# A two-block transformer kernel on one core: the S5 products with C issued four at a time into column groups, and the first attention's logits of two heads in turn on the halves of the rows

## The chip, the cores and the metric

The kernel runs on one core of a Trainium2 chip, as one launch. The metric is the device time of one execution in microseconds; lower is better. The host only lays the arrays out beforehand.

## The reference

Two transformer blocks run one after the other on 256 tokens of width 2048, in float32. Each has a wide input projection, several mixers, gates, an output projection and an MLP with a squared ReLU. What matters here are two mixers:

```
# block 1: attention with forget gates, 8 heads of 64
log_f  = log_sigmoid(f_logit + f_bias);  cum = cumsum(log_f)          # per token and head
logits = einsum('bqhd,bkhd->bhqk', q_block, k) * 64 ** -0.5
logits = logits + (cum[q] - cum[key]);  masked;  softmax;  @ v        # query blocks of 128

# block 2: S5, 64 groups of 16 channels, each with 64 complex states
s = scan(a, einsum('blgh,gph->blgp', u, bb))                          # complex, over the tokens
y = einsum('blgp,ghp->blgh', s_re, c_re) - einsum('blgp,ghp->blgh', s_im, c_im)
```

## The kernel before

Activations are kept transposed: features on the 128 partitions, tokens on the free axis. The bulk of the work is a stream of weight products. `run_stream` goes through 1048 steps; in step i ScalarE casts a 512 x 256 block of weights to its high part and VectorE subtracts it to get the low part (`split_step(i + 3)`, tile `w`, four buffers), evacuations that are due are issued (`run_late`), and TensorE multiplies the block of step i (`mm_step`, tile `ps`). Then `run_mixers` issues pieces of two generators, `chain_a` and `chain_b`, until a budget of VectorE time (1.42 us a step) is used up. So the order in each engine's queue is fixed when the program is built, and the mixers' products stand in TensorE's queue between steps of the stream.

A float32 product of the mixers is two passes on TensorE: the trace counts two MATMULs for each `mm` whose operands are plain float32, and one for each whose operands are float32r. All below count passes.

`attn1`, in `chain_a`, takes two heads at a time, r = 0 to 3. For each head hh of the pair it forms the logits in a bank of its own (`mx` tiles): for the two query blocks a product q k over 64 rows (head 0 on partitions 0 to 63, head 1 on 64 to 127), and a second product on the same columns that adds the row of minus the cumulated forget gates: a one-hot column of the identity against `ncr[0:8]`, over 8 rows. That is 16 passes for each r. `ncr` is made in `forget` from a product of 8 output columns, `pr`. Later in the same loop, the products with v of the two heads go to the two halves of one bank's partitions, each with 64 columns of stationary operand.

The S5 mixer, the second half of `chain_b`, goes through t = 0 to 31 (two groups each; kt = t // 4, q = t % 4). For each t VectorE rotates the inputs `bu` into `pa` and `pb`, runs two scans, and rotates back into `z0`, a `pz` tile out of two buffers. One t later, after the scans of t, `y(t - 1, z0)` multiplies it by 32 columns of C (`ct`), into partitions 32 q to 32 q + 31 of `yps`: two products, real and imaginary, four passes. Then `bu(t + 1)` follows, two passes. After four t VectorE reads `yps` (`y_out`), and GpSimd's queue loads the next `ct` when the old one is free, with the tables `tab` behind it.

`acc` and `sq2` are two tiles [128, 2, 256] that sum the squares for the norms; between the norm ahead of block 2 and the output projection of block 2 nothing else uses them.

Of the kernel before, what the change touches and what calls it, by code (L numbers as in the profile page):

```python
# [11 lines left out]
F32 = mybir.dt.float32  # L12
# [6 lines left out]
D = 2048          # model width  # L19
L = 256           # tokens  # L20
# [10 lines left out]
# Everything below keeps activations transposed: features on partitions, tokens on the free axis.  # L31
# A product x @ w with float32 accuracy takes three float32r passes: every operand is the exact sum
# of two float32r parts (hi, lo) and hi*hi + hi*lo + lo*hi is accumulated in PSUM.


class Group:
    """256 columns of a weight matrix against K rows, in steps of 512 rows.

    mode F: two accumulators, [w_hi x_hi + w_lo x_hi | w_hi x_lo]; T: the same with the tokens on the
    output partitions; M: one accumulator and 512 columns.  # L40
    """
# [7 lines left out]
class Build:  # L49
# [33 lines left out]
    def split(self, dst, k, n, src):  # L83
        """dst (r8 tile), k tiles k..k+n <- exact hi and lo parts of src [128, n, 256]."""
        hi = dst[:, k:k + n, 0]
        self.A.copy(hi, src)  # L86
        self.tt(dst[:, k:k + n, 1], src, hi.bitcast(F32), SUB)

    def split_scaled(self, dst, k, src, g):
        """dst k tile k <- parts of src [128, 256] times the per-partition g."""  # L90
        hi = dst[:, k, 0]
        self.act(hi, src, AF.Copy, scale=g)
        self.stt(dst[:, k, 1], src, g, hi.bitcast(F32), MUL, SUB)

# [164 lines left out]
    def first_work(self):  # L259
        """loads in the order of need, the split of x between those of the first weights"""  # L260
        I, S = self.I, self.S
        S.dma_start(self.T4[0], I["x"][0])
        S.dma_start(self.gs, I["gs"])
        self.load_unit(0, halves=True)
        self.V.memset(self.e32, E32)
        self.act(self.acc[:, 0, 0:32], self.e32, AF.Copy)
        S.dma_start(self.T4[1], I["x"][1])
        self.load_unit(1)
        S.dma_start(self.T4[2], I["x"][2])
        S.dma_start(self.T4[3], I["x"][3])  # L270
        S.dma_start(self.cst, I["cst"])
        self.load_unit(2)
        self.V.memset(self.mh, -0.5)
        self.open_b1()
        self.xg = self.R[0:4]
# [7 lines left out]
    def squares_x(self, j):  # L283
        """as squares(), on GpSimd: the other engines have no time for it at the start"""
        t = self.sgt("sqx")
        G = self.G
        G.tensor_tensor(t, self.T4[j], self.T4[j], op=MUL)
        if j == 0:
            G.tensor_tensor(self.acc, t[:, 0:2], t[:, 2:4], op=ADD)
        else:  # L290
            for h in range(2):
                G.tensor_tensor(self.acc, self.acc, t[:, 2 * h:2 * h + 2], op=ADD)
# [11 lines left out]
    def squares(self, x, first=False, last=False):  # L304
        """add x*x to acc; the last ones are left to the sum over the partitions"""
        if first:
            self.act(self.acc, x, AF.Square)
            return
        t = self.sq2 if last else self.ev("sq")
        self.act(t, x, AF.Square)  # L310
        if not last:
            self.tt(self.acc, self.acc, t, ADD)
# [4 lines left out]
    def norm(self, tag, fast=False):  # L317
        """rstd of the tokens, per token partition (rt) and as rows on all partitions (rbc)."""
# [30 lines left out]
    def hold(self, norm):  # L349
        """an evacuation waits for its norm, as long as the PSUM ring allows"""  # L350
        if norm not in self.have:
            self.held.append(norm)
            while norm not in self.have:
                yield 0.0
            self.held.remove(norm)

# [1 line left out]
    def ab(self, ps, name="ab"):  # L358
        """sum of the two accumulators"""
        t = self.ev(name)  # L360
        self.A.copy(t, ps[:, :, 1])  # L361
        self.tt(t, ps[:, :, 0], t, ADD)
        return t
# [60 lines left out]
    def evac_res(self, x, j, s, xg=None, gi=None, sq=True, flag=None, then=None):  # L424
        """x += product; then the parts of x*g for the next product and the squares for its norm"""
# [46 lines left out]
    def make_groups(self):  # L472
        R, T = self.R, self.T4
        # block 1
# [53 lines left out]
        # block 2  # L528
# [128 lines left out]
    def exp_acc(self, out, y, n):  # L657
        """exp(y) for [128, n] with a relative error of a few ulp"""
        self.G.tensor_tensor(out, self.e32[:, 0:n], y, op=ALU.pow)
        for _ in range(3):  # L660
            yield None
        t = self.p.tile([128, 32], F32, name="xa", tag="xa", bufs=1)[:, 0:n]
        self.ts(t, y, E32_FIX, 1.0, MUL, ADD)
        self.tt(out, out, t, MUL)

    def log1p_half(self, out, z, n):
        """log1p(z)/2 for 0 <= z <= 1, in place of an odd series in z/(2+z)"""
# [11 lines left out]
    # -- block 1  # L679
# [3 lines left out]
    def open_b1(self):  # L683
# [16 lines left out]
        self.cq, self.ncr, self.c2 = sm("cq", 16), sm("ncr", 256), sm("c2", 4)  # L700
        self.lf, self.rq, self.sm1 = sm("lf", 16), sm("rq", 32), sm("sm1", 32)
# [9 lines left out]
    def forget(self):  # L711
# [13 lines left out]
        # rows hi, lo of w by columns hi, lo of x: three of the four blocks add up to the product  # L725
# [26 lines left out]
        # coefficient of the recurrence, -4 softplus(-lambda)  # L752
# [16 lines left out]
        self.mm(pr[0:8, 0:128], lf[:, 0], self.U)  # L769
        self.mm(pr[0:8, 128:256], lf[:, 1], self.U, True, False)  # L770
        self.mm(pr[0:8, 128:256], lf[:, 0], self.ones, False, True)
        yield None
        self.V.tensor_copy(self.cq, ps[:, 0:16])
        self.act(self.ncr[0:8], pr[0:8, 0:256], AF.Copy, scale=-1.0)
# [102 lines left out]
    def attn1(self):  # L877
# [39 lines left out]
        for r in range(4):  # L917
            yield None
            pss = []
            for hh in range(2):  # L920
                h, hs = 2 * r + hh, slice(64 * hh, 64 * hh + 64)
                ps = self.mxt()
                hot = self.ident[0:8, h:h + 1].to_broadcast([8, 128])
                for o, ls, n in ((0, slice(0, 128), 128), (128, slice(128, 256), 256)):
                    self.mm(ps[:, o:o + n], q[hs, r, ls], kk[hs, r, 0:n], True, False)
                    self.mm(ps[:, o:o + n], hot, self.ncr[0:8, 0:n], False, True)
                pss.append(ps)
# [50 lines left out]
    # -- block 2  # L978
# [15 lines left out]
    def scatter(self, eng, dst, k, n, src):  # L994
        """[(q r), k, 256] of every src to its rows of dst [k, (src r), q, 256]"""
        for i, t in enumerate(src):
            for q in range(4):
                rs = slice(32 * q, 32 * q + 32)
                eng.dma_start(dst[k:k + n, 32 * i:32 * i + 32, q].rearrange("k r n -> r k n"), t[rs])

    def s5_params(self):
# [36 lines left out]
        # zero-order hold: k = (exp(lambda dt) - 1) / lambda  # L1038
# [55 lines left out]
        # exp(i theta t) for t < 256 by doubling, first 32 for all states at once  # L1094
# [110 lines left out]
    def gmlp(self):  # L1205
        # in the places of q and k, which the attention no longer needs
# [63 lines left out]
    def chain_b(self):  # L1270
        # The product with B contracts 16 channels only: the parts hi, lo of the input, for four
        # times 32 channels, go one below the other on 128 rows, and so do those of B
# [55 lines left out]
        def y(t, z):  # L1328
            kt, q = t // 4, t % 4
            if q == 0:  # L1330
                yps[kt] = self.p_mx.tile([128, 256], F32, name="yps", tag="yps", bufs=1)
            o = yps[kt][32 * q:32 * q + 32]
            for c in range(2):
                self.mm(o, ct[kt][:, c, q], z[:, c], c == 0, c == 1)
# [15 lines left out]
        z0 = None  # L1350
        for t in range(32):
# [14 lines left out]
            if t:  # L1366
                y(t - 1, z0)
# [6 lines left out]
            z0 = nt("pz", 2)  # L1374
# [11 lines left out]
        y(31, z0)  # L1386
# [31 lines left out]
def _tiles(w):  # L1418
    """[K, N] -> [N/512, 2, K/512] blocks of [128, 4, 256]: 512 rows by 256 columns, rows on partitions"""
# [5 lines left out]
def _cols(v):  # L1425
    """[n*128] -> [128, n]"""
# [3 lines left out]
def _layout(a):  # L1430
# [41 lines left out]
    sb = np.zeros((2, 64, 2, 32, 2, 16), f32)       # q, p, re/im, tau, q', channel  # L1472
    sc = np.zeros((8, 2, 64, 2, 4, 2, 16), f32)     # kt, q, p, re/im, tau%4, q', channel
# [27 lines left out]
```

## Time and profile before

| | |
|---|---|
| runs shown, median of 3 | 3115.57 us (3114.85 to 3116.56) |
| span of the profiled execution, first to last instruction | 3107.6 us |
| TensorE busy | 3079.1 us (99%) |
| VectorE busy | 2126.8 us (68%) |
| ScalarE busy | 1437.8 us (46%) |
| mean share of the 16 DMA engines, whole span | about 5 to 6 tenths |
| mean granted TensorE clock | 0.993 |

The page has the profiled execution's own time as its span alone; what lies around the span isn't in it. The median of the runs is 8.0 us above that span. A busy TensorE is one that has passes in flight; whether it gets through them at its best pace has to be read from starts of passes that follow each other.

### The profile page before, as it was taken

How to read it: one execution, taken by the hardware profiler on the slowest of the kernel's cores; microseconds unless marked ns; L12 is line 12 of the kernel's file. 1: busy time of each engine (PE TensorE's matmuls, PEld its weight loads, DVE VectorE, ACT ScalarE, POOL GpSimd, SP SyncE). 2: the span in 40 equal slices, each digit the busy share in tenths (PEclk: the TensorE clock that was granted, in tenths of full speed). 3: DMA queues.
4: the chain of work that ended last, by engine and by line, in shares of the span. 5: the costliest groups of instructions: out<-in, count | busy, mean ns of one | idle time of the engine just before them, and what ended most of it. 6: DMA issues, size and time to landing. Idle time of an engine off the chain costs nothing.

```text
span 3107.6 us, 43754 instructions
## 1 busy us (share of the span) xinstructions
PE 3079.1 (99%) x18072; PEld 2684.9 (86%) x18072; DVE 2126.8 (68%) x2607; ACT 1437.8 (46%) x1737; POOL 88.1 (3%) x115
## 2 busy tenths in 40 slices
PE   8999999999999999999999999999999999999998
PEld 6888889988888888888888888888998888888887
DVE  6765566566788976566678788886566656565565
ACT  4455444445544434344445554445444434344443
POOL 3000000000000000000000000000000000000000
PEclk9999999999999999999999999999999999999999
DMA  5554455565566665555675566655555555555553
GB/s 213 174 174 149 148 178 188 190 216 188 193 230 213 234 215 205 190 190 203 218 237 188 182 209 207 206 177 190 188 199 189 182 185 189 189 182 186 189 188 124
DMA packets 158567, 597.90 MB, mean 192 GB/s; under 512 B 11168, under 2 KB 13472, under 8 KB 158112
## 3 DMA queue, kind: packets, MB, share of 16 engines
q1 hardware_dynamic: 150464, 569.94, 52.9%
q0 software_dynamic: 7328, 24.12, 2.8%
q8 instruction: 142, 2.33, 0.3%
q10 hardware_dynamic: 576, 1.05, 0.1%
q14 instruction: 57, 0.47, 0.0%
HBM read 577.24 MB, written 17.83 MB: 191 GB/s over the span
## 4 chain that ended last, share of the span: by engine, by line
PE 75%; issue 23%; DVE 1%; DMA 0%; ACT 0%; SPq 0%; POOLq 0%; POOL 0%; DVEq 0%; ACTq 0%
PE ps L81 72%; PE mx L81 2%; PE yps L81 1%; PE bu L81 0%; DVE R L75 0%; DMA T<-in_x 0%; DVE w L66 0%; DVE T L66 0%; PE mx L958 0%; ACT w L130 0%; PE mx L1081 0%; SPq L117 0%; POOLq L1496 0%; POOL rt L315 0%; DVE ab L66 0%
## 5 line engine op out<-in xcount | busy, mean ns | idle before, releaser
L81 PE MATMUL ps<-R,w 128*128 128x256 f32 (+1 forms) x16768 | 2861.5, 333 | 15.0 <-DVE w L66 7.4
L81 PEld LDWEIGHTS ps<-R,w 128*128 128x128 f32 x16768 | 2507.7, 189 | 354.7 <-DVE w L66 8.8
L66 DVE TENSOR_TENSOR w<-raw,w 128x1024 fp32r<-128x1024 f32 x1048 | 1282.4, 1225 | 927.2 <-ACT w L130 926.4
L130 ACT CAST w<-raw 128x1024 fp32r<-128x1024 f32 x1048 | 1099.7, 1050 | 1557.0 <-PE ps L81 1383.2
L66 DVE TENSOR_TENSOR T<-T,ps 128x512 f32<-128x512 f32 x160 | 109.4, 684 | 9.1 <-PE ps L81 6.3
L81 PE MATMUL ps<-w,R 128*128 128x512 f32 (+1 forms) x640 | 114.2, 338 | 0.0
L81 PEld LDWEIGHTS ps<-w,R 128*128 128x128 f32 x640 | 97.5, 188 | 13.9
L66 DVE TENSOR_TENSOR ab<-ps,ab 128x512 f32<-128x512 f32 x154 | 105.3, 684 | 0.0
L361 ACT COPY ab<-ps 128x512 f32<-128x512 f32 x154 | 89.2, 579 | 0.0
L66 DVE TENSOR_TENSOR ab<-ab,rbc 128x512 f32<-128x512 f32 x120 | 83.1, 693 | 4.2
L315 POOL TENSOR_TENSOR rt<-nv,mh 128x2 f32<-128x2 f32 x5 | 3.5, 703 | 2022.7 <-DVE nv L72 2022.7
L66 DVE TENSOR_TENSOR R<-ab,R 128x512 fp32r<-128x512 f32 x68 | 46.6, 685 | 0.0
L86 ACT CAST R<-ab 128x512 fp32r<-128x512 f32 x68 | 41.8, 615 | 7.2 <-DVE ab L66 7.2
L75 DVE SCALAR_TENSOR_TENSOR ab<-ab 128x512 f32<-128x512 f32 x64 | 43.8, 684 | 0.0
L75 DVE SCALAR_TENSOR_TENSOR R<-T,gs,R 128x256 fp32r<-128x256 f32 x64 | 39.3, 660 | 4.0 <-ACT R L78 4.0
L1365 DVE TENSOR_TENSOR_SCAN pb<-magT,pa 128x256 f32<-128x256 f32 x64 | 40.7, 678 | 0.8
L78 ACT ACT_TABLE_LOAD x28 | 35.9, 1283 | 1.2 <-PEq L1492 0.7
L81 PE MATMUL yps<-pz,ct 128*32 128x256 f32 x128 | 33.6, 385 | 0.0
L78 ACT ACTIVATE R<-T,gs 128x256 fp32r<-128x256 f32 x64 | 28.5, 499 | 5.7 <-DMA T<-in_x 3.5
L1314 ACT CAST xs<-xk 128x256 fp32r<-128x256 f32 x32 | 12.9, 402 | 31.0 <-PE bu L81 29.9
L1307 POOL DMA_DIRECT2D tab<-dtab x32 | 17.7, 554 | 259.1 <-DVE pz L66 259.0
L66 DVE TENSOR_TENSOR pz<-pz,pa 128x256 f32<-128x256 f32 x64 | 24.2, 419 | 0.2
(217 smaller groups left out, 873.3 us busy)
## 6 DMA issues: line engine op xcount, KB each, us to landing
raw<-in_w_in SPq DMA_DIRECT2D x191, 1024.0 KB, 4.9
raw<-in_w_up SPq DMA_DIRECT2D x128, 1024.0 KB, 4.8
raw<-in_w_down SPq DMA_DIRECT2D x128, 1024.0 KB, 4.9
raw<-in_w_branch SPq DMA_DIRECT2D x40, 1024.0 KB, 4.9
raw<-in_w_out SPq DMA_DIRECT2D x32, 1024.0 KB, 4.9
dtab<-tb SPq DMA_DIRECT2D x16, 512.0 KB, 7.5
tab<-dtab POOLq DMA_DIRECT2D x32, 256.0 KB, 3.2
T<-in_x SPq DMA_DIRECT2D x8, 512.0 KB, 7.0
```

Of the source, the lines that this page charges most:

```text
L66: self.V.tensor_tensor(out, a, b, op=op)
L75: self.V.scalar_tensor_tensor(out, a, s, b, op0=op0, op1=op1)
L78: self.A.activation(out, a, func, **kw)
L81: self.T.matmul(out, lhsT, rhs, start=start, stop=stop, skip_group_check=True)
L86: self.A.copy(hi, src)
L130: self.A.copy(w[:, :, 0], raw)
L315: self.G.tensor_tensor(out, v, self.mh[:, 0:out.shape[-1]], op=ALU.pow)
L361: self.A.copy(t, ps[:, :, 1])
L1307: self.G.dma_start(tab[t], self.d_tab[t // 2][:, t % 2])
L1314: self.A.copy(xs[t], xk[kt][:, q])
L1365: self.V.tensor_tensor_scan(b[:, c], mg, a[:, c], 0.0, op0=MUL, op1=ADD)
```

## The change

It has two parts.

In S5, the states of four consecutive t are kept (`zs`), and when t % 4 is 0 and t is not, `y(kt - 1, zs)` issues the eight products of the four t at once: first the real parts of q = 0 to 3, then the imaginary ones, each q into its own 32 columns of the array. Since four states must live at once, q = 0 uses `acc`, q = 1 uses `sq2`, and q = 2 and 3 the two `pz` buffers.

In the first attention, both heads' products are issued in turn: q k of head 0 on rows 0 to 63, q k of head 1 on rows 64 to 127, then the two forget products. These now take 64 rows each, on the same halves: `ncr` is cleared to zero once, filled at partitions 0 to 7 and 64 to 71 (so `forget` makes `pr` twice and copies it twice), and the one-hot column is chosen on the half of its head.

Comments are taken out as well.

```diff
+        self.V.memset(self.ncr, 0.0)
...
-        self.mm(pr[0:8, 0:128], lf[:, 0], self.U)
-        self.mm(pr[0:8, 128:256], lf[:, 1], self.U, True, False)
-        self.mm(pr[0:8, 128:256], lf[:, 0], self.ones, False, True)
+        for o in (0, 64):
+            self.mm(pr[o:o + 8, 0:128], lf[:, 0], self.U)
+            self.mm(pr[o:o + 8, 128:256], lf[:, 1], self.U, True, False)
+            self.mm(pr[o:o + 8, 128:256], lf[:, 0], self.ones, False, True)
...
-        self.act(self.ncr[0:8], pr[0:8, 0:256], AF.Copy, scale=-1.0)
+        for o in (0, 64):
+            self.act(self.ncr[o:o + 8], pr[o:o + 8, 0:256], AF.Copy, scale=-1.0)
...
-            pss = []
-            for hh in range(2):
-                h, hs = 2 * r + hh, slice(64 * hh, 64 * hh + 64)
-                ps = self.mxt()
-                hot = self.ident[0:8, h:h + 1].to_broadcast([8, 128])
-                for o, ls, n in ((0, slice(0, 128), 128), (128, slice(128, 256), 256)):
-                    self.mm(ps[:, o:o + n], q[hs, r, ls], kk[hs, r, 0:n], True, False)
-                    self.mm(ps[:, o:o + n], hot, self.ncr[0:8, 0:n], False, True)
-                pss.append(ps)
+            pss = [self.mxt(), self.mxt()]
+            for o, ls, n in ((0, slice(0, 128), 128), (128, slice(128, 256), 256)):
+                for hh in range(2):
+                    hs = slice(64 * hh, 64 * hh + 64)
+                    self.mm(pss[hh][:, o:o + n], q[hs, r, ls], kk[hs, r, 0:n], True, False)
+                for hh in range(2):
+                    hs, h = slice(64 * hh, 64 * hh + 64), 64 * hh + 2 * r + hh
+                    hot = self.ident[hs, h:h + 1].to_broadcast([64, 128])
+                    self.mm(pss[hh][:, o:o + n], hot, self.ncr[hs, 0:n], False, True)
...
-        def y(t, z):
-            kt, q = t // 4, t % 4
-            if q == 0:
-                yps[kt] = self.p_mx.tile([128, 256], F32, name="yps", tag="yps", bufs=1)
-            o = yps[kt][32 * q:32 * q + 32]
+        def y(kt, zs):
+            yps[kt] = self.p_mx.tile([128, 256], F32, name="yps", tag="yps", bufs=1)
             for c in range(2):
-                self.mm(o, ct[kt][:, c, q], z[:, c], c == 0, c == 1)
+                for q, z in enumerate(zs):
+                    self.mm(yps[kt][32 * q:32 * q + 32], ct[kt][:, c, q], z[:, c], c == 0, c == 1)
...
-            if t:
-                y(t - 1, z0)
+            if t and q == 0:
+                y(kt - 1, zs)
+                zs = []
...
-            z0 = nt("pz", 2)
+            z0 = (self.acc, self.sq2)[q] if q < 2 else nt("pz", 2)
+            zs.append(z0)
...
-        y(31, z0)
+        y(7, zs)
```

On TensorE, the logits of one r (the second, r = 1) stand like this before; `mx<-T,T` is a product q k, `mx<-ncr,cst` one with the forget row, `ps` is the stream, and the size is that of the output:

```order
L81 MATMUL ps_2308<-R_74,w_2212 128x256
L81 MATMUL mx<-T_83,T_82 128x128
L81 MATMUL mx<-ncr,cst 128x128
L81 MATMUL mx<-T_83,T_82 128x256
L81 MATMUL mx<-ncr,cst 128x256
L81 MATMUL mx<-T_83,T_82 128x128
L81 MATMUL mx<-ncr,cst 128x128
L81 MATMUL mx<-T_83,T_82 128x256
L81 MATMUL mx<-ncr,cst 128x256
L81 MATMUL ps_2308<-R_75,w_2233 128x512
```

And like this with the change, between the same two products of the stream:

```order
L81 MATMUL ps_2313<-R_74,w_2217 128x256
L81 MATMUL mx<-T_83,T_82 128x128 x2
L81 MATMUL mx<-ncr,cst 128x128 x2
L81 MATMUL mx<-T_83,T_82 128x256 x2
L81 MATMUL mx<-ncr,cst 128x256 x2
L81 MATMUL ps_2313<-R_75,w_2238 128x512
```

The number of products is the same; the two of each row are now those of head 0 and head 1.

On TensorE in S5, the product with C of t = 3 and its surroundings before:

```order
L81 MATMUL ps_13299<-R_81,w_13289 128x512
L81 MATMUL ps_13299<-R_81,w_13289 128x256
L81 MATMUL yps<-pz,ct 32x256 x2
L81 MATMUL bu<-xs,ws 128x256 x2
L81 MATMUL ps_13423<-R_75,w_13323 128x512
```

And the same place with the change (`sq_92` is `sq2`), where the products of t = 0 to 3 now all stand:

```order
L81 MATMUL ps_13295<-R_81,w_13285 128x512
L81 MATMUL ps_13295<-R_81,w_13285 128x256
L81 MATMUL yps<-acc,ct 32x256
L81 MATMUL yps<-sq_92,ct 32x256
L81 MATMUL yps<-pz,ct 32x256 x2
L81 MATMUL yps<-acc,ct 32x256
L81 MATMUL yps<-sq_92,ct 32x256
L81 MATMUL yps<-pz,ct 32x256 x2
L81 MATMUL bu<-xs,ws 128x256 x2
L81 MATMUL ps_13426<-R_75,w_13319 128x512
```

At the three places ahead of this one, t = 0 to 2, the `yps` row is gone and `bu` follows the stream directly. Beside these places the queues of all engines hold the same instructions in the same order, apart from the names of the state tiles, one more MEMSET on VectorE at the start, and in `forget` three more products and one more copy on ScalarE.

## Rows read from the trace of the kernel before

**Rows 1.** Page: the span; the chain that ended last, by engine.

```profile
span 3107.6 us, 43754 instructions
...
PE 75%; issue 23%; DVE 1%; DMA 0%; ACT 0%; SPq 0%; POOLq 0%; POOL 0%; DVEq 0%; ACTq 0%
```

**Rows 2.** Waits of TensorE, whole span: total us, times, longest us.

```profile
PE ps L81 <- DVE w L66: 7.4, 3, 3.8
PE ps L81 <- ACT w L130: 7.3, 1, 7.3
```

**Rows 3.** Chain that ended last, in S5: start us, us, what (passes).

```profile
1583.69 0.24 PE bu L81 x2
...
1600.19 0.98 PE yps L81 x4
1601.17 0.43 PE bu L81 x2
...
2073.10 0.98 PE yps L81 x4
```

**Rows 4.** Chain that ended last, at the logits and one product with v.

```profile
255.15 4.15 PE mx L81 x16
...
279.93 0.81 PE mx L81 x8
...
322.50 5.09 PE mx L81 x16
...
359.62 4.68 PE mx L81 x16
```

**Rows 5.** TensorE in order of time, logits of r = 0: start us, us, passes.

```profile
255.08 0.49 PE L81 MATMUL mx<-T,T 64*128 64x128 f32 x2
255.49 0.48 PE L81 MATMUL mx<-ncr,cst 8*128 8x128 f32 x2
255.90 0.70 PE L81 MATMUL mx<-T,T 64*128 64x256 f32 x2
256.53 0.69 PE L81 MATMUL mx<-ncr,cst 8*128 8x256 f32 x2
```

**Rows 6.** Tile scr on TensorE: the products with v.

```profile
L81 PE MATMUL mx<-scr,T x32: 272/326/430, 279.9 to 390.8; 128*64 128x256 f32 x16, 128*64 128x128 f32 x16
```

**Rows 7.** In order of time, up to 279.8605, then up to 279.8725: passes begun.

```profile
279.86 0.43 PE L81 MATMUL mx<-scr,T 128*64 128x256 f32 x1
...
279.86 0.44 PE L81 MATMUL mx<-scr,T 128*64 128x256 f32 x2
```

**Rows 8.** Stretches at and after logits: busy us (instructions) by engine, granted clock, DMA.

```profile
255.00:259.20 4.20, 4.20 (x18) 2.34 (x16) 1.88 (x3) 1.04 (x1) 0.00 (x0) 1.00 0.25 52
...
291.30:294.70 3.40, 3.40 (x13) 2.83 (x12) 1.35 (x4) 0.00 (x0) 0.00 (x0) 0.51 0.00 0
...
325.50:332.30 6.80, 6.80 (x19) 4.82 (x20) 1.87 (x6) 0.00 (x0) 0.00 (x0) 0.50 0.13 53
...
363.10:369.80 6.70, 6.70 (x20) 5.28 (x20) 1.83 (x5) 0.00 (x0) 0.00 (x0) 0.50 0.05 19
```

**Rows 9.** S5 stretches: PE, PEld, DVE, ACT, POOL, clock, DMA.

```profile
1580.00:2080.00 500.00, 498.34 (x3008) 425.54 (x3007) 419.03 (x609) 252.70 (x342) 36.39 (x67) 1.00 0.59 197
1840.00:1960.00 120.00, 120.00 (x782) 105.00 (x781) 106.33 (x155) 59.01 (x81) 10.67 (x19) 1.00 0.60 203
```

**Rows 10.** In order of time, all engines, after the product of t = 19.

```profile
1914.83 1.05 PE L81 MATMUL yps<-pz,ct 128*32 128x256 f32 x4
...
1916.36 0.68 DVE L66 TENSOR_TENSOR pz<-pb,tab 128x512 f32<-128x512 f32 x1
```

**Rows 11.** In order of time, in forget, and VectorE at the start.

```profile
81.32 0.82 PE L81 MATMUL mx<-cst,lf 128*8 128x128 f32 x6
...
82.18 0.37 ACT L78 ACTIVATE ncr<-mx 8x256 f32<-8x256 f32 x1 [0.28 <-PE mx L81]
...
4.97 3.63 DVE L75 SCALAR_TENSOR_TENSOR R<-T,gs,R 128x256 fp32r<-128x256 f32 x4 [3.81 <-ACT R L78]
```

More of the change, by code (lines that the diff above doesn't have):

```diff
@@ L1349, in chain_b @@
         yield None
-        z0 = None
+        zs = []
         for t in range(32):
@@ L1365, in chain_b @@
                 self.V.tensor_tensor_scan(b[:, c], mg, a[:, c], 0.0, op0=MUL, op1=ADD)
-            if t:
-                y(t - 1, z0)
+            if t and q == 0:
+                y(kt - 1, zs)
+                zs = []
             if q == 0:
```

## The prediction

> **What bounds the kernel now.** I read the head of the page and its chain that ended last first: nearly all of that chain is TensorE, or issue time in which nothing is waited for [rows 1]. The waits of TensorE confirm it: its two largest sums are about 7 us each out of 3107.6 us, in four waits altogether [rows 2]. So the time is the length of TensorE's queue, and a change is worth what it takes out of that queue, at the place where it takes it, as long as VectorE keeps up.
>
> Then I read the chain at the two places of the change. In S5 every product with C stands in it: four passes take 0.98 us, and the `bu` behind takes 0.43 us where one with no such product ahead took 0.24 us [rows 3]. There are 32 of these products, each at 0.98. In the first attention the 16 passes of each r stand in it too, with 4.15 us for r = 0 and the same for r = 1, 5.09 for r = 2 and 4.68 for r = 3 [rows 4].
>
> **What one pass costs.** The logits of r = 0 in order of time give it [rows 5]. Two passes of 128 tokens go from one start to the next pair's in 0.41 us, two of 256 in 0.63. The 0.22 between them is two times 128 tokens, so a pass streams in 0.11 us per 128 tokens and 0.22 per 256. A pair of 128 then has 0.41 - 0.22 = 0.19 us that is no streaming, and it comes once for each pair, where the rows in use change from 64 to 8 or back. Check: 8 x 0.11 + 8 x 0.22 + 8 x 0.19 = 4.16, against 4.15. The S5 product fits as well: 4 x 0.22 = 0.88, and 0.10 of change on the way in; on the way out `bu` pays 0.43 - 0.24 = 0.19.
>
> **Do passes on different parts of the array run at once?** One place of the kernel before answers for columns. The products with v put two heads on the two 64-column halves, each with two passes of 256 and two of 128 tokens for every r [rows 6]. One after the other they would stream for 4 x 0.22 + 4 x 0.11 = 1.32 us; they took 0.81 with the changes included [rows 4]. And within 0.012 us of the first pass a second one of 256 tokens had begun [rows 7], which must be the other head's, since passes of one head can't start so close. The program writes all of head 0 ahead of head 1, so three unstarted passes were passed over.
>
> [...]
>
> **The change part by part.**
>
> S5. Removed: 32 x (0.98 + 0.19) = 37.4 us. In their place stand 8 batches of 16 passes, four in each column group. With the four groups at once a batch streams for 4 x 0.22 = 0.88, plus 0.10 on the way in, at most 0.04 for three later starts and 0.19 on the way out: 1.21 us, 9.7 in all. To start the fourth group TensorE must pass over three unstarted passes, as many as it did for v. Saved: 27.7 us. No row shows more than two groups, so the bounds are one pass at a time (16 x 0.22 + 0.29 = 3.8 us a batch, 30.5 in all, 6.9 saved) and all four. I take all four, since the groups are of the same kind as the two that the rows show.
>
> Logits. Removed: 4.15 + 4.15 + 5.09 + 4.68 = 18.1 us. All 16 passes now use 64 rows, so the seven changes inside an r go, and the two halves of the rows write two banks. With both halves at once an r takes 4 x 0.11 + 4 x 0.22 = 1.32, plus one change of 0.19: 1.5 us, 6.0 in all, 12.1 saved. Halves of rows never stand next to each other in the trace before; the nearest row is again that of v. The lower bound is nothing saved, if the 0.19 belongs to products on part of the rows and not to the change, and the halves take turns.
>
> Clock. [...] What r = 2 and 3 lost inside the logits is in the sum already (5.09 and 4.68); outside, half of 3.4, of 4.7 (327.6 to 332.3) and of 5.5 (364.3 to 369.8) is lost, 6.8 us. What TensorE did before each fall was some 3 to 4 us of passes on 64 or 8 rows. The S5 products, 1.2 us at a time, leave the clock at 1.00 throughout [rows 9]. At 1.5 us an r is nearer to these, so I take all 6.8 as saved, with 0 as the other bound.
>
> `forget`. Six passes of 8 columns are added to six that took 0.82 us; they lie in another column group, so I take 0.2 of at most 0.8. The second copy, 0.37 us on ScalarE [rows 11], delays only ScalarE there. The MEMSET falls in the first 5 us, where VectorE waits for its first input until 4.97 [rows 11]. Both at nothing.
>
> New waits. In S5 VectorE now writes `acc` at t = 4, 8, ... right after the batch that reads it was issued; the two-buffer `pz` gave it one t more. At t = 20, the tightest of these places, that write began at 1916.36, and the product of t = 19 had ended at 1914.83 + 0.98 = 1915.81 [rows 10]: 0.55 us to spare, of which the longer batch uses 0.04. Were it late, the next weight split would queue behind it on VectorE, and TensorE meets that only once its three steps of ready weights are used up. The next `ct` load waits for the end of the batch as it did for the last product, with the table loads behind it on GpSimd's queue, at most 0.04 us later.
>
> Sum: -27.7 - 12.1 - 6.8 + 0.2 = -46.4 us. The profiled span of 3107.6 would become 3061.2. The page gives no time around it; I leave the 8.0 us by which the median lies above the span as they are: 3115.6 - 46.4 = **3069.2 us**, 1.5% faster. A difference of under 0.2%, 6.2 us, would not be told from no change.
>
> **Rivals.**
>
> 1. Not all four column groups at once. If two at a time, a batch has 8 rounds of 0.22 and takes 2.1 us; if passes start strictly in order, both passes of q hold up q + 1, which makes 9 rounds, 2.3 us. 8 batches cost 16.6 or 18.2 us instead of 9.7: 3076 to 3078 us. The products with v speak against strict order, nothing speaks for or against four. [...] Chance 0.14.
>
> 2. Halves of rows take turns. Streaming stays 2.64 us and one change is left, 2.8 us for an r: 6.8 saved instead of 12.1, and between 0 and 6.8 of the clock, since runs of 2.8 us lie between those that lowered it and those that didn't: 3074 to 3081; with the 0.19 still paid by each pair, 3088. Chance 0.13; together with the first, 3081 to 3090, 0.05.
>
> 3. VectorE becomes the bound in S5. It is busy 419 of 500 us, and 106.3 of 120 in the fullest stretch [rows 9]; with 27.7 us less that is 89%, and with about 7 us less there 94%. Against it: no wait of TensorE for VectorE worth naming there, and 6% left. If the stretch from 1840 on (235 us) kept its pace, 13 us of the gain would be lost: 3082. Chance 0.05.
>
> 4. Slower: the clock. If passes neither overlap in columns nor in rows, a batch is 3.8 us of passes on 32 columns, as long as the logits that lowered the clock. A fall of 6.8 us after each of 8 batches costs 8 x 3.4 = 27 us against 6.9 saved; with logits at 2.8 us and their falls unchanged (-6.8), the end is 3115.6 - 6.9 + 27.2 - 6.8 = 3129. It decides from about five such falls on. Chance 0.03.
>
> **How the numbers follow.** The forecast has the remaining 0.60, with a range of its own of 3063 to 3074 (the clock's other falls shift by one or two, overheads of a batch are off by half a microsecond). The range for all is 3062 to 3088: it takes in the first three rivals and leaves out the fourth, the worst of the second and a bit below. Faster by over 0.2% is everything but the fourth and part of an unforeseen mix: 0.95; within 0.2%: 0.02; slower: 0.03.
>
> **What would show each step.** In the changed profile: 8 groups of 16 `yps` passes in the chain of about 1.0 us each, and `bu` at 0.24 behind the stream at the other 24 places; 16 `mx` passes in about 1.5 us for each r; a granted clock of 1.00 from 255 to 375 us; VectorE's share in S5 near 89% without new waits of TensorE. Batches of 2 us or logits of 2.8 would make the prediction wrong by the amounts above, and falls of the clock behind the batches by more.

## The result and the profile after

The change takes 3064.1 us (median of 4 runs, 3063.0 to 3076.2) against 3115.2 before (median of 4, 3101.8 to 3116.6); the ratio is 0.9855, 95% interval 0.9838 to 0.9872. The forecast was 3069.2. In four more runs of the change, with seven of before beside them, the ratio was 0.9849 (0.9824 to 0.9873). The profiled execution of the change has a span of 3074.1 us and took 3076.2, the longest of the first four. So 2.1 us lie around the span, not the 8.0 that the prediction left there, and the profiled execution of before stands for a run of about 3109.7.

The page still says that TensorE's queue is the time [rows 1]:

```profile
span 3074.1 us, 43760 instructions
...
PE 75%; issue 23%; DVE 1%; DMA 0%; ACT 0%; SPq 0%; POOLq 0%; POOL 0%; DVEq 0%; ACTq 0%
```

The chain that ended last, in S5 (start us, us, passes), to be read against [rows 3]:

```profile
1596.55 0.23 PE bu L81 x2
...
1632.44 1.00 PE yps L81 x16
1633.44 0.43 PE bu L81 x2
...
2040.37 1.00 PE yps L81 x16
```

Sixteen passes take 1.00 us where four took 0.98, and the chain has eight such pieces. `bu` without a product ahead of it takes 0.23 us.

TensorE in order of time at the first batch:

```profile
1632.37 0.40 PE L81 MATMUL yps<-acc,ct 128*32 128x256 f32 x1
1632.38 0.40 PE L81 MATMUL yps<-sq,ct 128*32 128x256 f32 x1
1632.38 0.41 PE L81 MATMUL yps<-pz,ct 128*32 128x256 f32 x2
1632.61 0.38 PE L81 MATMUL yps<-acc,ct 128*32 128x256 f32 x1
```

The first passes of all four states begin within 0.02 us of each other, and the next round begins 0.24 us later. The written order has both passes of `acc` first.

The chain at `forget`, where 12 passes took 1.32 us before (0.82 of it in [rows 11]), and at the first two of the four logits, against [rows 4]:

```profile
82.90 1.55 PE mx L81 x18
...
257.44 1.51 PE mx L81 x16
...
286.07 1.51 PE mx L81 x16
```

The stretches of the attention and of S5 (PE, PEld, DVE, ACT, POOL busy, granted clock, DMA share, GB/s), against [rows 8, 9]:

```profile
250.00:400.00 150.00, 150.00 (x971) 131.66 (x970) 92.82 (x126) 80.56 (x118) 0.00 (x0) 1.00 0.47 166
...
1580.00:2043.00 463.00, 461.32 (x2951) 409.34 (x2950) 414.04 (x606) 247.72 (x338) 36.45 (x67) 1.00 0.62 209
...
1840.00:1960.00 120.00, 120.00 (x815) 108.80 (x814) 111.71 (x164) 59.15 (x82) 12.28 (x23) 1.00 0.65 218
```

The clock is at 1.00 through the attention. VectorE is busy 414 of 463 us in S5, which now ends at 2043, and 111.7 of 120 in the fullest part, and TensorE waits for it no more than before there. Its largest waits over the whole span are at the start (total us, times, longest us):

```profile
PE ps L81 <- DVE R L75: 8.4, 1, 8.4
PE ps L81 <- DVE w L66: 7.5, 3, 4.5
```

**Where the profile's difference went.** The spans differ by 33.5 us only, not by the 46.4 of the forecast. The missing part is in neither of the changed places. Between the attention and S5 stands a long piece of the first MLP without products of mixers. Its passes in a stretch of 580 us, first before, then with the change:

```profile
920.00:1500.00 580.00, 580.00 (x3348) 507.21 (x3348) 420.75 (x533) 252.61 (x276) 0.00 (x0) 1.00 0.61 206
```

```profile
920.00:1500.00 580.00, 580.00 (x3285) 503.02 (x3284) 410.89 (x515) 249.55 (x275) 0.00 (x0) 1.00 0.59 203
```

3348 passes against 3285, at a granted clock of 1.00 in both and with no waits: a step of 16 passes takes 2.774 us in one profile and 2.826 in the other. By the starts of the steps this holds for some 245 steps, about 13 us. In the second MLP both profiles go at the slower pace (3398 and 3399 passes in the 600 us from 2400 to 3000).

Both profiles have the same 17408 passes of the stream, so the rest can be read by setting the start of the same pass in one against its start in the other. Ahead of the logits the change is 2.3 us late (254.3 us before, 256.6 with it): 0.2 for `forget` and 2.1 from the start of the kernel, where the granted clock was at 0.50 once more, for 3.4 us (27.4 to 30.8 us). Behind the attention it is 16.7 us early, ahead of S5 3.6 early, behind S5 32.7 early, and so it stays up to the stream's last pass. So the attention gave 19.0 us, the MLP took back 13.1, S5 gave 29.1, and 0.8 came behind the last pass. The two changed places and `forget` together are worth 47.9 us, 1.5 more than forecast. The other three runs of the change, at 3063.0 to 3064.3, are 12 to 13 us under the profiled one.

### The profile page after: what moved, and what is told of

Its sections match the earlier page's. It is cut to its first block, busy times and chain, and to the rows that moved or that the text cites. A ratio compares the mean times of both kernels' runs of the same rounds, so it can differ in the third digit from the quotient of the medians.

```text
span 3074.1 us, 43760 instructions
## 1 busy us (share of the span) xinstructions
PE 3044.4 (99%) x18078; PEld 2672.3 (87%) x18078; DVE 2124.9 (69%) x2608; ACT 1436.8 (47%) x1738; POOL 88.1 (3%) x115
## 4 chain that ended last, share of the span: by engine, by line
PE 75%; issue 23%; DVE 1%; DMA 0%; ACT 0%; SPq 0%; POOLq 0%; POOL 0%; DVEq 0%; ACTq 0%
PE ps L81 73%; PE mx L81 2%; DMA T<-in_x 0%; PE bu L81 0%; PE yps L81 0%; DVE w L66 0%; DVE R L75 0%; DVE T L66 0%; PE mx L962 0%; ACT w L130 0%; PE mx L1085 0%; ACT R L78 0%; SPq L117 0%; POOLq L1502 0%; POOL rt L315 0%
## 5 line engine op out<-in xcount | busy, mean ns | idle before, releaser
L66 DVE TENSOR_TENSOR pa<-pa,pb 128x256 f32<-128x256 f32 x64 | 24.2, 419 | 0.1
L66 DVE TENSOR_TENSOR bb<-tb,cs 128x128 f32<-128x128 f32 (+2 forms) x48 | 22.5, 469 | 1.3
L66 DVE TENSOR_TENSOR tb<-bb 128x128 f32<-128x128 f32 (+2 forms) x48 | 22.5, 468 | 1.2
```

The source lines that it names most:

```text
L66: self.V.tensor_tensor(out, a, b, op=op)
```

## The experiments

Durations are those of the chain that ended last, unless another view is named.

**Each part alone.** The S5 part with the old logits:

```diff
...
-        self.V.memset(self.ncr, 0.0)
...
-            pss = [self.mxt(), self.mxt()]
+            pss = []
+            for hh in range(2):
+                h, hs = 2 * r + hh, slice(64 * hh, 64 * hh + 64)
+                ps = self.mxt()
+                hot = self.ident[0:8, h:h + 1].to_broadcast([8, 128])
...
```

> The S5 part alone; the logits and forget as before. Theory (columns at once): the eight batches take 1.00 us each in the chain with 0.19 behind them, so 32 x 1.17 - 8 x 1.19 = 27.9 us come off, and the logits of the four r stay at 4.15 us or more with the granted clock at 0.5 after two or three of them. Time about 28 us under before, 0.991 of it. Rival (the gain of the whole change came mostly from the logits and the clock, or the two parts need each other): under 20 us off. A third thing to watch: the 224 steps without mixers from about 0.9 to 1.5 ms go at either 2.774 or 2.826 us a step in the profiles so far; if that is chance of the execution and not of the program, it may stand at either here, 12 us apart.

3081.2 us against 3114.3, ratio 0.989 (0.9868 to 0.9912), 33 us, with the interval from 27 to 41. The batches took 1.00 us, and the MLP went at 2.774 us a step. The old logits in the chain, then a stretch in and behind the second r (the clock is the first of the three numbers behind the engines):

```profile
258.47 4.15 PE mx L81 x16
291.45 5.42 PE mx L81 x16
328.62 5.14 PE mx L81 x16
365.74 4.73 PE mx L81 x16
```

```profile
294.10:300.70 6.60, 6.60 (x18) 4.49 (x18) 2.23 (x7) 0.00 (x0) 0.00 (x0) 0.50 0.18 74
```

Here the granted clock fell to 0.50 after all four r (263.4 to 266.6, 294.1 to 300.7, 331.6 to 338.2 and 369.2 to 375.8 us); the line is that of the second. The S5 part stands by itself. By the stream's passes S5 is 29.1 us shorter here too, while the forecast's 27.7 lies at the lower end of the interval.

The attention part with the old S5:

```diff
...
-            if t and q == 0:
-                y(kt - 1, zs)
-                zs = []
+            if t:
+                y(t - 1, z0)
...
-            z0 = (self.acc, self.sq2)[q] if q < 2 else nt("pz", 2)
...
+            z0 = nt("pz", 2)
...
```

> The attention part alone; S5 as before. Theory: each r takes 1.51 us in the chain, the granted clock stays at 1.00 from 250 to 385 us, and 12 us of passes and up to 7 us of clock come off: 17 to 19 us under before, 0.994. The 32 products with C stay at 0.98 us. Rival (the clock's falls move elsewhere, since the same array rows are idle for the rest of the attention): about 12 us under before, with stretches at 0.5 somewhere between 250 and 385 us.

3090.9 us against 3114.3, ratio 0.9923 (0.9905 to 0.9942): 23 us, with the interval from 18 to 30, where 17 to 19 were expected. The chain at an r and at a product with C, and the clock from 250 to 400:

```profile
255.67 1.51 PE mx L81 x16
...
1594.17 0.98 PE yps L81 x4
```

```profile
250.00:400.00 150.00, 150.00 (x971) 131.69 (x970) 93.23 (x126) 81.42 (x120) 0.00 (x0) 1.00 0.49 169
```

The passes are as expected and no fall appeared elsewhere. By the stream's passes the attention is 19.1 us shorter in this profile, as in that of the whole change, so the surplus is not in the attention itself. It is probably the clock's, since most runs of before seem to have had more falls than its profile; the next section works that out. Because of it the two parts' 33 and 23 us add up to more than the 48 to 51 of the whole change, while 29.1 and 19.1 agree with its profile.

**What overlaps with what.** The logits written head by head, on 64 rows each:

```diff
-            for o, ls, n in ((0, slice(0, 128), 128), (128, slice(128, 256), 256)):
-                for hh in range(2):
-                    hs = slice(64 * hh, 64 * hh + 64)
+            for hh in range(2):
+                hs, h = slice(64 * hh, 64 * hh + 64), 64 * hh + 2 * r + hh
+                hot = self.ident[hs, h:h + 1].to_broadcast([64, 128])
+                for o, ls, n in ((0, slice(0, 128), 128), (128, slice(128, 256), 256)):
...
```

> As the change, but the logits are written head by head: all four products of head 0 on rows 0 to 63, then all four of head 1 on rows 64 to 127. Nothing is left out. Theory (a half of the rows passes over what waits for the other half, as the heads of the products with v did on columns): 16 passes in about 1.5 us again, starts of the two heads some 10 ns apart. Rival (passes start in the order written, and the turn-taking of the change is what makes them overlap): head 1 starts only after head 0's last pass has begun, 16 passes in about 2.6 to 2.8 us.

2.06 us for each r (the chain names 13 of the 16 passes):

```profile
256.90 2.06 PE mx L81 x13
```

Neither of the two. In the starts of the passes, head 1 began with head 0's fifth of eight, 0.55 us in, and then ran beside it: 0.55 + 1.51 = 2.06. At that moment three of head 0's passes were waiting. That suggested a limit of three waiting passes, to be tested below.

A batch written state by state:

```diff
-            for c in range(2):
-                for q, z in enumerate(zs):
+            for q, z in enumerate(zs):
+                for c in range(2):
```

> As the change, but a batch of S5 is written state by state: real and imaginary product of q = 0, then both of q = 1, and so on, so that the first pass of the last group stands behind twelve passes, nine of which would have to be passed over. Nothing is left out. Theory (groups go on independently, however deep): 16 passes in 1.00 us. Rival 1 (strict order): each group's first pass starts with the last pass of the group before, 13 rounds of 0.22, about 2.9 us. Rival 2 (only some few waiting passes can be passed over): in between, 1.4 to 2.2 us, with the last groups starting late.

1.02 us a batch, with all four states' first passes together although nine passes stood ahead of the last one unstarted (chain, then TensorE in order of time):

```profile
1633.85 1.02 PE yps L81 x16
```

```profile
1633.78 0.40 PE L81 MATMUL yps<-acc,ct 128*32 128x256 f32 x1
1633.79 0.40 PE L81 MATMUL yps<-sq,ct 128*32 128x256 f32 x1
1633.80 0.42 PE L81 MATMUL yps<-pz,ct 128*32 128x256 f32 x2
```

So the limit, if there is one, is not over the whole queue: here each group has exactly three passes waiting. The test of it, six passes of head 0 ahead of head 1:

```diff
...
+            for hh in range(2):
+                logit(hh, 128)
+                forget(hh, 128)
+                logit(hh, 256)
+            for hh in range(2):
+                forget(hh, 256)
```

> As the change, but head 0 has its first three products (six passes) written together, then head 1 its first three, then the last of each. Nothing is left out. Theory (each part of the array lets three passes wait besides the one at work, and the next one holds up all that is written behind it; read from the run written head by head, where head 1 began with head 0's fifth of eight passes, 0.55 us in): head 1 begins with head 0's third pass, 0.33 us in, and an r takes 1.51 + 0.33 = 1.84 us. Rival 1 (halves of rows need turns of one product): more than 2.06. Rival 2 (it is a count over the whole queue, not by part): 9 passes could be passed over in S5, so all six can be here, and an r takes 1.51.

1.835 us by the starts of the passes, the same for all four r; the chain (which names 15 of the 16) and TensorE in order of time:

```profile
259.74 1.83 PE mx L81 x15
```

```profile
259.67 0.49 PE L81 MATMUL mx<-T,T 64*128 64x128 f32 x2
260.00 0.27 PE L81 MATMUL mx<-ncr,cst 64*128 64x128 f32 x1
260.00 0.37 PE L81 MATMUL mx<-T,T 64*128 64x128 f32 x1
```

Head 1's first q k pass, the last row, begins 0.33 us in, with head 0's third pass, as the theory said to the hundredth. Both rivals fall.

**What a change of the rows in use costs.** The forget products back on 8 rows of each half, in turn:

```diff
-                    hs, h = slice(64 * hh, 64 * hh + 64), 64 * hh + 2 * r + hh
-                    hot = self.ident[hs, h:h + 1].to_broadcast([64, 128])
+                    hs, h = slice(64 * hh, 64 * hh + 8), 64 * hh + 2 * r + hh
+                    hot = self.ident[hs, h:h + 1].to_broadcast([8, 128])
```

> As the change, but the forget products keep 8 rows each, at partitions 0 to 7 and 64 to 71, while the q k products keep their 64: the heads still take turns, and the rows in use change within an r (64, 8, 64, 8). Nothing is left out. Theory (0.19 for each change of the rows in use, and both heads at once otherwise): 1.32 + 4 x 0.19 = 2.1 us for an r, against 1.51; the clock stays at 1.00. Rival (the 0.19 was not the change but a price of products on few rows, or the two heads' 8-row products don't run at once): 2.6 us or more.

```profile
257.13 2.10 PE mx L81 x16
```

```profile
250.00:400.00 150.00, 150.00 (x955) 129.81 (x954) 91.38 (x124) 80.16 (x118) 0.00 (x0) 1.00 0.48 162
```

2.10 against 1.51: three more changes, 0.20 each, and both heads still at once. The clock stayed at 1.00, although half of the passes were on 8 rows again.

**What lowered the clock.** The logits three times over:

```diff
-            for o, ls, n in ((0, slice(0, 128), 128), (128, slice(128, 256), 256)):
+            for o, ls, n in 3 * ((0, slice(0, 128), 128), (128, slice(128, 256), 256)):
```

> As the change, but the logits of each r are formed three times over into the same place (the last stands, so nothing is left out): 48 passes on both halves of the rows, 3 x 1.32 + 0.19 = 4.15 us in the chain, the length that the logits had before the change. Theory 1 (the clock fell because the logits took so long without full use of the array): the granted clock falls to 0.5 again after two or three of the four r. Theory 2 (it fell because at any moment only 64 or 8 rows were at work; with both halves at work an r of this length does no harm): the clock stays at 1.00 from 250 to 385 us, and the change's gain in clock came from the overlap, not from the shorter time.

```profile
255.44 4.13 PE mx L81 x48
```

```profile
250.00:400.00 150.00, 150.00 (x1033) 132.10 (x1032) 88.43 (x121) 75.97 (x114) 0.00 (x0) 1.00 0.45 155
```

As long as before the change, and no fall: the length alone is not it. Then head 0 alone, three times, with head 1 behind:

```diff
-            for o, ls, n in ((0, slice(0, 128), 128), (128, slice(128, 256), 256)):
-                for hh in range(2):
+            for hh in (0, 0, 0, 1):
...
+                for o, ls, n in ((0, slice(0, 128), 128), (128, slice(128, 256), 256)):
```

> As the change, but head 0's four logit products are written three times over and then head 1's once (nothing is left out; the last copy stands): 24 passes on rows 0 to 63 alone, one behind the other without a change of the rows in use, about 3.2 us before head 1 may begin beside them; some 4.6 us for an r. Theory 1 (the clock fell because at any moment only part of the rows was at work): it falls to 0.5 again after some of the four r. Theory 2 (it fell because of the idle 0.19 at each of the eight changes of the rows in use, together 1.5 of the 4.15 us): no change inside, so it stays at 1.00.

```profile
255.68 4.68 PE mx L81 x30
```

```profile
250.00:400.00 150.00, 150.00 (x951) 131.69 (x950) 86.48 (x119) 74.94 (x112) 0.00 (x0) 1.00 0.43 150
```

No fall with only one half of the rows at work for most of 4.68 us. Left are the changes of the rows in use, and the passes on 8 rows. The order of before the change, with the forget products on all 128 rows:

```diff
...
+            for hh in range(2):
+                hs, h = slice(64 * hh, 64 * hh + 64), 64 * hh + 2 * r + hh
+                hot = self.ident[:, h:h + 1].to_broadcast([128, 128])
...
+                    self.mm(pss[hh][:, o:o + n], hot, self.ncr[:, 0:n], False, True)
```

> As the change, but the logits are written as before the change, head by head and product by product in turn, with the forget products on all 128 rows instead of 8 (nothing is left out): the rows in use change from 64 to 128 and back eight times for each r, and no pass has fewer than 64 rows. Theory (0.19 for each change; passes on different numbers of rows don't run at once): 2.64 + 8 x 0.19 = 4.15 us an r. For the clock, theory 1 (the idle at the changes lowered it): 0.5 after some of the four r, as before the change. Theory 2 (the passes on 8 rows did): 1.00 throughout from 250 to 385 us.

```profile
255.26 4.17 PE mx L81 x16
```

```profile
250.00:400.00 150.00, 150.00 (x908) 128.07 (x907) 89.16 (x122) 76.56 (x114) 0.00 (x0) 1.00 0.46 155
```

4.17 us, eight changes, no overlap: nearly the time of before the change (3.89 us from the first pass to the stream's next one, where before took 4.15; on the way out the rows in use stay 128), and still 1.00. So in long runs the passes on 8 rows are what is left. Each of these runs is one execution, though, and by its time and clock (3101.2 to 3101.8 us, 0.996) about one run of before in five seems to have had no fall at the logits either (5 of 26; an estimate, since they have no trace). That long runs of passes without 8 rows never lowered the clock rests on three kernels with four r each, against seven falls at the eight r of before and of the S5 part alone.

Few rows are not the only thing that stands ahead of a fall. In the profile of before the granted clock is also at 0.51 behind another mixer's 32 small products, which use all 128 rows and stream two tokens each (TensorE in order of time, then the stretch behind):

```profile
218.12 3.63 PE L81 MATMUL mx<-pk,scr 128*128 128x2 f32 x32
```

```profile
223.00:226.50 3.50, 3.50 (x13) 3.01 (x12) 0.00 (x0) 0.57 (x1) 3.50 (x1) 0.51 0.68 280
```

With the change the same 32 products begin at 220.40 us and take 3.63 us as well, and the granted clock behind them is 0.50 from 225.4 to 228.8 us. Falls differ from one execution to the next, though: the runs of before have mean granted clocks from 0.991 to 0.996.

The fourth rival, one column group for long:

```diff
-            for c in range(2):
-                for q, z in enumerate(zs):
+            every = list(enumerate(zs))
+            for c, some in 4 * [(0, every[:1]), (1, every[:1])] + [(0, every[1:]), (1, every[1:])]:
+                for q, z in some:
```

> As the change, but in each batch of S5 the state q = 0 is multiplied four times over (16 passes in one column group), and then the other three groups follow (nothing is left out). Theory (three waiting passes for each part of the array): the others begin with the 13th pass, 2.6 us in, so a batch takes 2.6 + 1.0 = 3.6 us in the chain. The fourth rival of the prediction says that such a length of passes on 32 columns lowers the clock: then 0.5 shows behind several of the eight batches; else the clock stays at 1.00 throughout S5 and the rival had no ground.

```profile
1631.96 3.61 PE yps L81 x28
```

```profile
1580.00:2080.00 500.00, 498.32 (x3157) 435.31 (x3156) 425.46 (x615) 259.14 (x349) 36.53 (x67) 1.00 0.60 199
```

3.61 us as worked out from three waiting passes, and the clock at 1.00 behind all eight batches. The fall that the rival foresaw did not come, in one execution with one group alone at work for 2.6 us of each batch; 3.8 us of it were not run.

**The stream's pace.** The change once more, unaltered:

> The change once more, unaltered, for its spread and its pace. Theory: the 224 steps of the stream around 0.9 to 1.5 ms stand at 2.774 or at 2.826 us from one execution to the next, so runs lie near 3063 or near 3076 us, and this profile may show either; the batches are 1.00 us and the logits 1.51 in any case. Ratio to before 0.984 to 0.987. Rival (the changed program itself has the slower pace, through where it puts its tiles or its instructions): 2.826 again, and all runs near 3076.

```profile
920.00:1500.00 580.00, 580.00 (x3285) 503.01 (x3284) 411.65 (x516) 249.32 (x274) 0.00 (x0) 1.00 0.60 204
```

The profile has the slower pace again and took 3077.6 us; the three others took 3063.3 to 3066.2. And the run head by head once more, also unaltered:

> The run written head by head once more, with times, for the pace of the stream's 224 steps around 0.9 to 1.5 ms. If the pace is chance of an execution, its profile may show 2.774 or 2.826 us a step and its runs lie near 3066 or 3078; if it is a property of the program when it is profiled, the profile shows 2.774 again. Logits 2.06 us an r in any case; against the change's runs near 3064 it should lie 4 x 0.55 = 2.2 us higher.

```profile
920.00:1500.00 580.00, 580.00 (x3348) 507.03 (x3347) 418.90 (x526) 253.82 (x280) 0.00 (x0) 1.00 0.61 206
```

The faster pace again, 3067.7 us (3064.2 to 3069.7; the change's own spread is as wide as the 2.2 us looked for). So each of these two programs repeated its pace when profiled, while the change's six other runs are all without the 13 us. In this stretch the two profiles of the change have 3285 passes, and those of before, of each part alone, of both runs head by head and of the run with six passes ahead have 3348 to 3351. The slower pace seems to occur without the change too: two of the 26 runs of before (3124.5 and 3125.8 us) lie 12 to 16 us above the others that are listed with the same mean clock of 0.993. Neither plain chance nor the program alone fits; what sets the pace stays open.

## Why the prediction was right

**What bounds the kernel** held. What was taken out of TensorE's queue came off the time: the 32.7 us that the stream is ahead behind S5 are still there at its last pass. No other engine took over: VectorE at 89% of S5 and at 93% in its fullest part (89% and 94% forecast), without new waits.

**S5.** The batches came out at 8 x (1.00 + 0.19) = 9.5 us, where the forecast had 9.7. S5 got 29.1 us shorter, against 27.7: the 32 products taken out were worth 1.2 us each and not the 1.17 of the sum. Where that rest lies stays open. The step that carried it, from two column groups in the products with v to four in the batch, was an extension beyond the rows, and it held. The wait for `acc` did not show. The order from which the forecast argued is confirmed by the run state by state: products on different parts need not be written in turn to overlap. With three passes of each part waiting, the batch written state by state took 1.02 us, where one that starts in the order written would take 2.9, an estimate of 13 rounds of 0.22. With more ahead, head 1 began when three of the passes ahead of it were left to start: 0.33 us in with six ahead and 0.55 with eight.

**Logits** came out at 1.51 us for each r, against 1.5. The price of 0.19 for a change of the rows in use, read from [rows 5], was confirmed by the runs with 8 rows in turn (three more changes, 0.59) and with 128 rows (4.17 us in the chain, against the 4.15 worked out). `forget` grew by 0.23, against 0.2.

**Clock.** The outcome was right, the argument is not shown, and the size was off. The prediction had the clock saved because an r becomes short. The runs fit that, but they fit another cause as well: the change also widened the forget products from 8 to 64 rows, a side of it that the prediction counted only for the changes of rows that it removes. With the passes still on 8 rows, but the heads in turn and an r of 2.10 us, the clock stayed at 1.00; with no passes on 8 rows and an r of 4.13 to 4.68 us it stayed there too. Only in the kernels with both, passes on 8 rows and an r of 4.15 us, did it fall, to 0.50 or 0.51. So either side of the change, the turns that shorten an r or the wider passes, seems to be enough, with one execution behind each of these runs. Which of them the chip answers to stays open.

The size: the profile of before had 8.3 us of falls at the logits (1.5 inside them, and 6.8 outside, an estimate: half of the time at a granted clock of 0.50 or 0.51 in [rows 8]). No run shows the 6.8 by itself; the attention came out 19.0 us shorter, of which 4 x (4.15 - 1.51) = 10.6 are passes, so that 8.4 are left for all the falls. But the profile of before was a short execution. The runs of before that seem to have none lie at 3101.5, so the median of 3115.2 would hold 13.7 us of them, 5.4 more than the profile; this is an estimate, since those runs have no trace. From 3101.5, 29.1 + 4 x (4.15 - 1.51) - 0.2 = 39.5 us lead to 3062.0, 1 to 4 us under the place where six of the change's eight runs lie (3063.0 to 3066.2). The forecast took this term from one execution and carried it over to the median, with the 8.0 us that were thought to lie around the span. That is probably where most of the 5 us between forecast and result come from.

**The pace** of the MLP was not in the forecast at all. It hid about 13 us of the gain in the profile and none in most runs; the range would have covered it in a run like the profiled one (3076.2). That the profiles' difference without the pace comes to 46.5 us, the forecast's sum, is chance: S5 gave 1.4 more, and the start of the kernel took 2.1.

## What to carry to other kernels

Products on some columns or some rows of the array cost next to nothing extra here when their neighbours in the queue used the other ones: four S5 products took 1.00 us where one took 0.98, and 16 passes on the two halves of the rows 1.51 where they would stream for 2.64 one after the other (an estimate from [rows 5]). So collect such products until all parts have work, and write few passes of a part before the next part's first: four cost nothing to speak of (1.02 us for a batch), six cost 0.33 us (1.84 for 1.51). Keep the rows in use the same through a run of small products, widening a narrow one with zeros if need be, since every change cost about 0.2 us here. And compare profiles stretch by stretch before their spans: a stretch that the change never touched moved by 13 us.

## What the runs showed of the hardware

- Passes on different column groups, and on the two halves of the rows, ran at once (16 `yps` passes in 1.00 us, 16 `mx` passes in 1.51). Written one part after the other, the later part began when three of the passes ahead of it were left to start: with head 0's fifth of eight, 0.55 us in (2.06 us for an r), and with its third of six, 0.33 us in (1.84); with four ahead in each of the column groups it began at once (1.02 us for a batch). A batch with sixteen ahead in one column group took 3.61 us, as worked out from three waiting.
- 16 passes that take 4.15 us at a granted clock of 1.00, half of them on 8 rows, stood at or ahead of every fall to 0.50 or 0.51 at the logits (7 of 8 r). Behind runs of 4.1 to 4.7 us with 64 rows or more it stayed at 1.00 in three kernels, and so it did with 2.10 us and half of the passes on 8 rows. Another 3.63 us of products on all 128 rows, two tokens each, stood ahead of a fall to 0.50 or 0.51 in the profiles of before and of the change.
- A change of the rows in use cost 0.19 to 0.20 us each time (64 to 8 and back, 64 to 128 and back).
- The dense stream went at two steady paces at a granted clock of 1.00 and without waits, 2.774 and 2.826 us for the same 16 passes, each for some 245 steps in one profile. What sets the pace was not found.
